# A batched 64x64 matmul: one input loads ahead of the other, two more loads of the other move to ScalarE's queue, ScalarE's order changes, the last tile gets PSUM of its own, and there is one more result buffer

## Chip, cores, metric

One core of a Trainium2 chip. The metric is the device time of one execution in microseconds (us), the median of several. All runs quoted here are fast: none was over 1.5% above the fastest of its kernel. Times in tables of instructions count from the start of the profiled span. The profiled span is shorter than the timed execution by about 2 us. In the lines of the profile DVE is VectorE, ACT is ScalarE, PE is TensorE, POOL is GpSimd and SP is SyncE; the digits in their rows of slices are busy tenths.

## The reference

```python
def setup_inputs():
    return {
        "a": np.random.randn(1024, 64, 64).astype(np.float32),
        "b": np.random.randn(1024, 64, 64).astype(np.float32),
    }

def reference(a, b):
    return np.matmul(a, b).astype(np.float32)
```

There are 1024 products of 64x64 matrices. Inputs are 2 x 16.78 MB, the result 16.78 MB: 50.33 MB over HBM.

## The kernel before

b and the result go in 16 tiles of 64 products (1 MB each), a in 8 tiles of 128 products (2 MB each, read as fp32 and written to SBUF as bf16 by the DMA). I number tiles from 0, so tile 15 is the last of b and of the result, and tile 7 the last of a.

For each tile of the result, VectorE "spreads" the transposed a into a block-diagonal operand, ScalarE casts b to bf16, TensorE multiplies, and the two halves of the result are evacuated (copied to SBUF) from PSUM, where the products are accumulated, the first by ScalarE, the second by VectorE. For each tile of a, VectorE "regroups" it, TensorE transposes it and ScalarE copies the transposes to SBUF. Loads of a and stores of the result are issued by GpSimd and share one DMA queue. Loads of b are issued by SyncE, two of them by ScalarE.

```python
    A_AHEAD = 3; B_AHEAD = 4; N_BD = 2; HOLD = 2
    ...
    o_pool = ctx.enter_context(tc.tile_pool(name="o_pool", bufs=5))
    t_psum = ...(tc.tile_pool(name="t_psum", bufs=4, space=bass.MemoryType.PSUM))
    o_psum = ...(tc.tile_pool(name="o_psum", bufs=2, space=bass.MemoryType.PSUM))
    ...
    def load_a(s):
        a_sb = a_pool.tile([128, 4, 16, 64], bf16, name="a_sb")
        for h in range(4):
            nc.gpsimd.dma_start(out=a_sb[:, h, :, :]..., in_=a_v[s, h])

    def load_b(t):
        b_sb = b_pool.tile([128, 16, 128], fp32, name="b_sb")
        queue = nc.scalar if t in (1, 3) else nc.sync
        queue.dma_start(out=b_sb[:], in_=b_v[t])
    ...
    def multiply(t, between):
        ...
        for half in range(2):
            o_ps = o_psum.tile([128, 4, 2, 2, 64], fp32, name="o_ps")
            for g8 in range(8):
                ...  # 4 matmuls
                if last and g8 % 4 == 3:      # last tile: evacuate quarters
                    gl = g8 // 4 * 2
                    copy = nc.vector.tensor_copy if gl else nc.scalar.copy
                    evacuate(o_ps, 4 * half + gl, gl, 2, copy)
            if not last:
                copy = nc.vector.tensor_copy if half else nc.scalar.copy
                evacuate(o_ps, 4 * half, 0, 4, copy)
            if half == 0:
                between()
        ...  # the tile's store, kept back; the last tile's in quarters

    def advance(t):
        if t + 1 < n_t:
            cast(t + 1)
        if t + B_AHEAD < n_t:
            load_b(t + B_AHEAD)

    with tc.manual_schedule():
        load_a(0)
        for t in range(B_AHEAD):
            load_b(t)
        for bd in bd_tiles:
            nc.vector.memset(bd[:], 0.0)
        ...
        for t in range(n_t):
            s, half = t // 2, t % 2
            if t + 1 < n_t:
                spread(t + 1)
            if half == 0:
                ...  # regroup(s + 2), load_a(s + 4)
            multiply(t, lambda: advance(t))
            ...  # transposes for the next tiles of a
            if t >= HOLD - 1:
                store(t - HOLD + 1)
        ...
```

## Time and profile before

| | before |
|---|---|
| time, median (range) | 139.34 us (139.12 to 139.62) |
| profiled span | 137.7 us |
| VectorE busy | 109.4 us (79%) |
| ScalarE busy | 87.1 us (63%) |
| TensorE matmuls busy | 67.6 us (49%) |
| HBM traffic | 50.33 MB |

Two things are nearly full, and a share of the whole span hides both. First the page's slices: VectorE's and the DMA engines' busy tenths, and what the engines moved in each fortieth of the span.

```profile
DVE  5770034959899999999999999999999999968440
...
DMA  2999999999999999999999999999999999992592
GB/s 61 305 305 308 305 280 260 209 251 273 236 251 298 383 283 267 358 394 356 271 278 387 396 317 268 305 403 390 398 396 400 389 396 389 384 367 106 177 337 100
```

The DMA row is full from the second slice to the 36th (about 124 us), dips, and recovers for the last stores. The GB/s row seems to say that the early slices are slower, but it counts what was written: the loads of a write half of what they read.

The table by stretches of the same kernel (time, then busy us of TensorE, its weight loads, VectorE, ScalarE and GpSimd, granted clock, DMA share, GB/s) puts VectorE beside it:

```profile
60.00:80.00 20.00, 11.87 (x216) 11.02 (x216) 19.35 (x28) 15.31 (x20) 7.13 (x7) 0.82 1.06 345
80.00:100.00 20.00, 13.00 (x218) 12.39 (x216) 19.35 (x27) 15.93 (x21) 4.09 (x3) 0.76 1.05 346
100.00:120.00 20.00, 10.20 (x192) 9.82 (x189) 19.34 (x28) 14.95 (x20) 3.77 (x4) 0.67 1.03 392
120.00:125.00 5.00, 3.62 (x70) 3.51 (x68) 3.86 (x7) 3.46 (x6) 1.09 (x1) 0.50 0.94 357
125.00:130.00 5.00, 2.26 (x40) 2.04 (x38) 3.58 (x7) 2.56 (x7) 1.59 (x2) 0.50 0.25 80
```

VectorE is busy 19.35 of every 20 us, and the DMA engines have no room either, until 125 us. Then the DMA share drops to 0.25.

The start, from the timeline of VectorE (start, duration, instruction, count, idle time before it and what ended it):

```profile
17.17 1.23 DVE L80 COPY a_bf<-a_sb 128x4096 bf16<-128x4096 bf16 x1 [7.76 <-DMA a_sb<-in_a_dram]
...
31.26 1.23 DVE L80 COPY a_bf<-a_sb 128x4096 bf16<-128x4096 bf16 x1 [1.75 <-DMA a_sb<-in_a_dram]
...
35.89 3.09 DVE L102 COPY at_bd<-at_sb 32x1024 f32<-32x1024 f32 x4 [0.59 <-ACT at_sb L92]
```

The first regroup (a's tile 0) is at 17.17 us, the third (a's tile 2) at 31.26 us. From the spread of tile 2 at 35.89 us VectorE runs without a gap for 86.4 us. I call this VectorE's chain.

The end, same view, with GpSimd's issues of stores (POOL):

```profile
119.20 3.10 DVE L102 COPY at_bd<-at_sb 32x1024 f32<-32x1024 f32 x4
...
123.35 0.76 DVE L118 CAST b_bf<-b_sb 128x512 bf16<-128x512 f32 x2 [1.05 <-DMA b_sb<-in_b_dram]
...
124.12 2.79 DVE L146 COPY o_sb<-o_ps 64x512 f32<-64x512 f32 x4
...
127.47 1.59 POOL L135 DMA_DIRECT2D out_dram<-o_sb  x2 [6.38 <-ACT o_sb L146]
...
131.55 1.73 DVE L146 COPY o_sb<-o_ps 64x256 f32<-64x256 f32 x4 [1.74 <-PE o_ps L154]
133.58 0.72 POOL L135 DMA_DIRECT2D out_dram<-o_sb  x1 [2.04 <-DVE o_sb L146]
```

Read it so: the chain's last spread ends at 122.3 us; VectorE waits 1.05 us for b's tile 15; it evacuates its half of tile 14 until 126.9. In the packets, the DMA engines are without load or store from 125.50 to 128.93 us, and the last packet of a store ends at 135.84.

### The profile page before, as it was taken

The page shows a single profiled execution, that of the slowest core. Times are in us where ns is not written, and L with a number is a line of the kernel's source. Part 1 is how long each engine was busy: PE and PEld are TensorE (multiplying, and loading weights), DVE is VectorE, ACT ScalarE, POOL GpSimd, SP SyncE. Part 2 cuts the span into 40 slices and gives each one's busy share as a digit, 9 for nine tenths or more (in the row PEclk, how much of TensorE's full clock was granted, in tenths as well). Part 3 has the DMA queues.
Part 4 walks back from the last instruction along what each step waited for, and adds up shares of the span by engine and source line. Part 5 has one row for each costly group of instructions (what it writes and reads, how often), then busy time and mean ns, then how long its engine had stood idle before and what let it go on. Part 6 is the DMA issues. An engine that isn't in the chain of part 4 may idle for free.

```text
span 137.7 us, 2820 instructions
## 1 busy us (share of the span) xinstructions
PE 67.6 (49%) x1152; PEld 63.9 (46%) x1152; DVE 109.4 (79%) x144; ACT 87.1 (63%) x120; POOL 43.3 (31%) x57
## 2 busy tenths in 40 slices
PE   0000063295857375629563679297229743374510
PEld 0000062295856375619563569296229643373510
DVE  5770034959899999999999999999999999968440
ACT  1030029049899998986799578864996794576400
POOL 6811141743543054205163330213020303210640
PEclk9999999658699959995999555959955995555555
DMA  2999999999999999999999999999999999992592
GB/s 61 305 305 308 305 280 260 209 251 273 236 251 298 383 283 267 358 394 356 271 278 387 396 317 268 305 403 390 398 396 400 389 396 389 384 367 106 177 337 100
DMA packets 17468, 42.12 MB, mean 306 GB/s; under 512 B 1072, under 2 KB 1072, under 8 KB 17456
## 3 DMA queue, kind: packets, MB, share of 16 engines
q0 software_dynamic: 9008, 25.17, 64.4%
q1 hardware_dynamic: 7392, 14.68, 29.8%
q10 hardware_dynamic: 1056, 2.10, 4.1%
q8 instruction: 9, 0.15, 0.4%
q14 instruction: 3, 0.02, 0.0%
HBM read 33.55 MB, written 16.78 MB: 366 GB/s over the span
## 4 chain that ended last, share of the span: by engine, by line
DMA 27%; DVE 20%; SPq 16%; issue 12%; PE 9%; ACT 9%; POOL 3%; POOLq 1%; DVEq 0%; ACTq 0%
SPq L74 16%; DMA b_sb<-in_b_dram 16%; DVE at_bd L102 11%; DMA a_sb<-in_a_dram 10%; DVE o_sb L146 8%; PE at_ps L89 5%; PE o_ps L154 4%; ACT b_bf L113 4%; ACT o_sb L146 3%; ACT at_sb L92 2%; DVE a_bf L80 2%; POOL out_dram L135 2%; POOL a_sb L66 1%; POOLq L241 1%; DVEq L80 0%
## 5 line engine op out<-in xcount | busy, mean ns | idle before, releaser
L154 PE MATMUL o_ps<-b_bf,at_bd 128*128 128x64 bf16 x1024 | 47.0, 217 | 40.4 <-ACT b_bf L113 16.5
L154 PEld LDWEIGHTS <-at_bd 128*128 128x128 bf16 x1024 | 44.9, 114 | 43.8 <-issue 22.5
L102 DVE COPY at_bd<-at_sb 32x1024 f32<-32x1024 f32 x64 | 47.3, 739 | 6.6 <-ACT at_sb L92 4.7
L146 DVE COPY o_sb<-o_ps 64x512 f32<-64x512 f32 (+1 forms) x68 | 44.7, 657 | 4.0 <-PE o_ps L154 1.7
L146 ACT COPY o_sb<-o_ps 64x512 f32<-64x512 f32 (+1 forms) x68 | 37.7, 555 | 14.9 <-PE o_ps L154 11.5
L135 POOL DMA_DIRECT2D out_dram<-o_sb x19 | 20.8, 1096 | 64.9 <-DVE o_sb L146 34.6
L89 PE MATMUL at_ps<-identity,a_bf 128*128 128x128 f32 x128 | 24.1, 353 | 23.4 <-DVE a_bf L80 23.4
L89 PEld LDWEIGHTS at_ps<-identity,a_bf 128*128 128x128 f32 x128 | 20.1, 187 | 23.6 <-issue 23.6
L92 ACT COPY at_sb<-at_ps 128x512 f32<-128x512 f32 x32 | 17.9, 588 | 19.4 <-PE at_ps L89 19.1
L113 ACT CAST b_bf<-b_sb 128x2048 bf16<-128x2048 f32 x15 | 28.5, 1899 | 2.5 <-DMA b_sb<-in_b_dram 2.2
L66 POOL DMA_DIRECT2D a_sb<-in_a_dram x32 | 21.9, 689 | 25.8 <-DMA a_sb<-in_a_dram 22.5
L80 DVE COPY a_bf<-a_sb 128x4096 bf16<-128x4096 bf16 x8 | 9.8, 1227 | 9.7 <-DMA a_sb<-in_a_dram 9.5
L186 DVE MEMSET at_bd<- 128x4096 f32 x2 | 6.9, 3472 | 2.5 <-PEq L230 1.7
L92 ACT ACT_TABLE_LOAD x1 | 1.3, 1283 | 4.8 <-issue 4.8
L74 ACT MOVE_SHAPE b_sb<-in_b_dram x2 | 0.6, 320 | 1.7 <-issue 0.9
L118 DVE CAST b_bf<-b_sb 128x512 bf16<-128x512 f32 x2 | 0.8, 424 | 1.0 <-DMA b_sb<-in_b_dram 1.0
L120 ACT CAST b_bf<-b_sb 128x512 bf16<-128x512 f32 x2 | 1.1, 616 | 0.0
masks.py:199 POOL TENSOR_SCALAR_AFFINE_SELECT identity<-identity 128x128 f32<-128x128 f32 x1 | 0.3, 289 | 0.1
masks.py:197 POOL MEMSET identity<- 128x128 f32 x1 | 0.3, 268 | 0.0
L230 POOL MEMSET const-float32-0.0<- 128x1 f32 x1 | 0.1, 93 | 0.3 <-issue 0.3
L230 POOL MEMSET const-bfloat16-1.0<- 128x1 bf16 x1 | 0.1, 96 | 0.0
L230 POOL MEMSET const-uint8-127<- 128x1 uint8 x1 | 0.1, 96 | 0.0
(1 smaller groups left out, 0.1 us busy)
## 6 DMA issues: line engine op xcount, KB each, us to landing
out_dram<-o_sb POOLq DMA_DIRECT2D x15, 1024.0 KB, 16.9
a_sb<-in_a_dram POOLq DMA_DIRECT2D x32, 256.0 KB, 15.6
out_dram<-o_sb POOLq DMA_DIRECT2D x4, 256.0 KB, 4.8
b_sb<-in_b_dram SPq DMA_DIRECT2D x14, 0.5 KB, 20.2
b_sb<-in_b_dram ACTq DMA_DIRECT2D x2, 0.5 KB, 18.8
```

The costliest lines, as they stand in the source:

```text
L66: nc.gpsimd.dma_start(out=a_sb[:, h, :, :].rearrange("p v k -> p (v k)"), in_=a_v[s, h])
L74: queue.dma_start(out=b_sb[:], in_=b_v[t])
L80: nc.vector.tensor_copy(a_bf[:], a_sb[:].rearrange("p h v k -> p v h k"))
L89: nc.tensor.transpose(at_ps[:, vo, :], a_cols[:, 4 * vo + 2 * j + wl, :], identity[:])
L92: nc.scalar.copy(at_tiles[s][:, j, :, wl, :, :], at_ps[:].rearrange("p vo (g mp) -> p g mp vo", mp=4),)
L102: nc.vector.tensor_copy(bd[rows, :, :, :, h, :].rearrange("p j g wl mo -> p j (g wl) mo"), at_tiles[t // 2][rows, :, half, :, :, :].rearrange(
L113: nc.scalar.copy(b_bf[:], b_sb[:])
L135: nc.gpsimd.dma_start(out=o_v[t, :, lo : lo + n, :], in_=o_sb[:, lo : lo + n].rearrange("p gh j wl n -> p (gh j wl n)"),)
L146: copy(dst, src)
L154: nc.tensor.matmul(o_ps[:, g8 // 2, g8 % 2, j, :], at_bd[:, j, g, :, u], b_bf[:, g, 64 * u : 64 * u + 64], start=(u == 0), stop=(u == 1),)
L186: nc.vector.memset(bd[:], 0.0)
L241: with _tile.TileContext(nc) as tc:
```

## The change

Its intent: let compute start sooner (a's first tile loads alone, and b waits until half of it has landed), feed TensorE sooner (casts ahead of the evacuations on ScalarE), let more loads and stores be in flight (tiles 5 and 7 of b on ScalarE's queue too, six result buffers), and shorten the end (the last tile's quarters in four PSUM banks of their own). One of two memsets goes from VectorE to GpSimd.

```diff
-    o_pool = ctx.enter_context(tc.tile_pool(name="o_pool", bufs=5))
+    o_pool = ctx.enter_context(tc.tile_pool(name="o_pool", bufs=6))
...
-        queue = nc.scalar if t in (1, 3) else nc.sync
-        queue.dma_start(out=b_sb[:], in_=b_v[t])
+        queue = nc.scalar if t in (1, 3, 5, 7) else nc.sync
+        load = queue.dma_start(out=b_sb[:], in_=b_v[t])
+        if t < 2:
+            tc.add_manual_dep(load.ins, first_a[1].ins.name, ...)  # waits for it
...
         for half in range(2):
-            o_ps = o_psum.tile([128, 4, 2, 2, 64], fp32, name="o_ps")
+            if not last:
+                o_ps = o_psum.tile([128, 4, 2, 2, 64], fp32, name="o_ps")
             for g8 in range(8):
+                if last and g8 % 4 == 0:
+                    o_ps = t_psum.tile([128, 2, 2, 2, 64], fp32, name="at_ps")
...
-            if half == 0:
-                between()
...
-        for bd in bd_tiles:
-            nc.vector.memset(bd[:], 0.0)
+        nc.vector.memset(bd_tiles[0][:], 0.0)
...
+        nc.gpsimd.memset(bd_tiles[1][:], 0.0)
...
                 spread(t + 1)
+                cast(t + 1)
+            if t + B_AHEAD < n_t:
+                load_b(t + B_AHEAD)
...
-            multiply(t, lambda: advance(t))
+            multiply(t)
```

More of the change, by code (lines that the diff above doesn't have):

```diff
@@ L60 @@
     a_tiles, b_tiles, abf_tiles, at_tiles, bbf_tiles = {}, {}, {}, {}, {}
-    held = {}
+    held, first_a = {}, []
     def load_a(s):
@@ L65, in load_a @@
         for h in range(4):
-            nc.gpsimd.dma_start(
+            load = nc.gpsimd.dma_start(
                 out=a_sb[:, h, :, :].rearrange("p v k -> p (v k)"), in_=a_v[s, h]
             )
+            if s == 0:
+                first_a.append(load)
         a_tiles[s] = a_sb
@@ L72, in load_b @@
         b_sb = b_pool.tile([128, 16, 128], fp32, name="b_sb")
-        queue = nc.scalar if t in (1, 3) else nc.sync
-        queue.dma_start(out=b_sb[:], in_=b_v[t])
+        queue = nc.scalar if t in (1, 3, 5, 7) else nc.sync
+        load = queue.dma_start(out=b_sb[:], in_=b_v[t])
+        if t < 2:
+            tc.add_manual_dep(
+                load.ins,
+                first_a[1].ins.name,
+                mybir.DependencyInfo(
+                    mybir.DependencyClass.Sync, mybir.DependencyReason.DATA
+                ),
+                reason="first tile of a goes ahead",
+            )
         b_tiles[t] = b_sb
@@ L125, in store, with multiply @@
             piece()
-    def multiply(t, between):
+    def multiply(t):
         at_bd = bd_tiles[t % N_BD][:].rearrange("p j g wl h mo -> p j g (wl h mo)")
@@ L138, in put, with evacuate @@
             )
-        def evacuate(o_ps, gh, gl, n, copy):
+        def evacuate(o_ps, gh, n, copy):
             for par in range(2):
                 for wl in range(2):
-                    src = o_ps[64 * wl : 64 * wl + 64, gl : gl + n, par, :, :]
+                    src = o_ps[64 * wl : 64 * wl + 64, :, par, :, :]
                     dst = o_sb[64 * par : 64 * par + 64, gh : gh + n, :, wl, :]
@@ L148, in multiply @@
         for half in range(2):
-            o_ps = o_psum.tile([128, 4, 2, 2, 64], fp32, name="o_ps")
+            if not last:
+                o_ps = o_psum.tile([128, 4, 2, 2, 64], fp32, name="o_ps")
             for g8 in range(8):
+                if last and g8 % 4 == 0:
+                    o_ps = t_psum.tile([128, 2, 2, 2, 64], fp32, name="at_ps")
                 g = 8 * half + g8
+                gl = (g8 % 4 if last else g8) // 2
                 for j in range(2):
@@ L154, in multiply @@
                         nc.tensor.matmul(
-                            o_ps[:, g8 // 2, g8 % 2, j, :],
+                            o_ps[:, gl, g % 2, j, :],
                             at_bd[:, j, g, :, u],
@@ L161, in multiply @@
                 if last and g8 % 4 == 3:
-                    gl = g8 // 4 * 2
-                    copy = nc.vector.tensor_copy if gl else nc.scalar.copy
-                    evacuate(o_ps, 4 * half + gl, gl, 2, copy)
+                    copy = nc.scalar.copy if g8 == 3 else nc.vector.tensor_copy
+                    evacuate(o_ps, g // 4 * 2, 2, copy)
             if not last:
                 copy = nc.vector.tensor_copy if half else nc.scalar.copy
-                evacuate(o_ps, 4 * half, 0, 4, copy)
-            if half == 0:
-                between()
+                evacuate(o_ps, 4 * half, 4, copy)
         if last:
@@ L173, in multiply @@
             held[t] = [lambda: put(0, 8)]
-    def advance(t):
-        if t + 1 < n_t:
-            cast(t + 1)
-        if t + B_AHEAD < n_t:
-            load_b(t + B_AHEAD)
     with tc.manual_schedule():
```

## The prediction

> **What bounds the kernel now.** Two things run nearly full. (1) DMA: the page's slices show the DMA row at 9 from the second slice to about 123 us. HBM traffic is 33.55 + 16.78 = 50.33 MB. Counting the trace's packets in 4 us windows (a's at the 4 KB that they read), the sum is 392 to 418 GB/s from 5 to 118 us: about 126 us of DMA work, beginning at 2.4 us. (2) VectorE: the table by stretches has it busy 9.7 of every 10 us between 40 and 120 us; per tile 3.09 us of spreads, 2.80 of evacuation, half of a 1.23 us regroup: 6.5 us. PE and ACT have slack. The timeline shows this VectorE chain starting when a's third tile lands (regroup at 31.26 us) and running without a gap to 122.3. Ends: the first tile of a lands at 17.05 us (it shares the engines with b); after 122.3 VectorE loses about 4 us to waits (cast of the last b 1.05, last evacuations 1.17 and 1.74), and the DMA engines idle from 125.5 to 128.9.
>
> **What changes, costed.**
> - Start. a's first packets start at 4.7 us, b's at 2.4. Tile 0 of a alone (2 MB at 400 GB/s) lands near 11 us instead of 17; first transposes 6 us sooner. But about 2.3 us of b traffic (0.7 MB) is given up: about -1.8 us of DMA work. The first three tiles of a and four of b (10.5 MB) land together near 31 us whatever their order, and VectorE's third regroup waits for that: expected at 31.5 to 33 us (31.26 before), so the continuous VectorE chain starts no sooner.
> - One 3.47 us memset leaves VectorE for GpSimd: it lay in waiting time, worth nothing.
> - Casts ahead: PE's waits for the cast (16.5 us in the table of waits) shrink; PE isn't the limit: about 0.
> - Tiles 5 and 7 of b on ACT's queue. The Trainium skill ("DMA: Bandwidth & Descriptors", Queues, rings and completion order) says each DMA engine goes round the queues packet by packet; the trace agrees: per 4 us a moved 0.77 MB against 0.84 for b on two queues, but about 1.02 against 0.55 on one. So b runs ahead by about 8 us: the last b tile lands near 115 us, not 122.9, and the wait for b at the end (2.2 + 1.05 us) goes. Stores lag some 5 us instead; six buffers absorb that.
> - Own PSUM banks: the last tile's matmuls no longer wait (1.6 + 1.6 us) for evacuations; its last evacuation ends near 130.5 instead of 133.3.
>
> **Sum.** VectorE could end 3 us sooner. But stores alone run at only about 330 GB/s (128.9 to 135.8 us), against 397 mixed with loads. With b done at 115, about 6.6 MB of stores remain: 20 us, ending near 135, plus 1.9 us to the end of the span. The DMA tail takes back much of the gain: span about 136 against 137.7, time about 137.6 us (-1.2%).
>
> **Would show it right:** first regroup near 11 us; third still at 31 to 33; last b cast no longer waiting; last tile's matmuls in one unbroken group; DMA idle gap before the last stores shorter than 1.5 us; VectorE still 97% busy from 40 to 120.
>
> **Would make it wrong:** a's third tile landing well before 31 us (more gain, 135); ACT blocked while issuing b loads, or casts blocking evacuations that wait behind them (a loss); a's later tiles lagging so far behind b that regroups wait.
>
> Chances: faster by over 2% 0.25, within 2% 0.70, slower 0.05. Range 135.5 to 139.5 us.

## The result, and the profile after

| | before | after |
|---|---|---|
| time, median (range) | 139.34 us (139.12 to 139.62) | 137.12 us (136.94 to 137.30) |
| ratio, 95% interval | | 0.984 (0.9817 to 0.9863) |
| profiled span | 137.7 us | 134.8 us |
| VectorE busy | 109.4 us | 105.0 us |
| first packet of a / of b | 4.69 / 2.40 us | 2.68 / 11.30 us |
| last packet of a / of b | 90.2 / 122.9 us | 95.3 / 114.6 us |
| end of the store of result tile 5 | 92.8 us | 98.3 us |
| HBM traffic done by 100, 120, 125 us | 38.56, 46.36, 48.18 MB | 38.46, 46.38, 48.18 MB |

A ratio is the mean time of one kernel's fast runs over that of the other's of the same rounds, so it isn't quite the ratio of the medians. The change is 1.6% faster, and the interval lies clear of 1. The time lies in the predicted range, 0.5 us under the predicted 137.6.

The last row is the most telling: for 125 us both kernels move the same bytes in the same time. What the change gained lies behind that.

The slices of the kernel after:

```profile
DVE  5512099069999999997999999997599999999900
...
DMA  2999999999999999999999999999999999998593
GB/s 19 185 204 261 309 305 301 309 308 279 272 294 311 312 394 346 303 275 361 393 360 273 272 381 396 340 267 288 393 394 396 393 399 395 407 406 350 191 320 136
```

The stretches, with the same columns:

```profile
60.00:80.00 20.00, 14.84 (x251) 14.05 (x248) 18.60 (x26) 17.68 (x26) 6.42 (x8) 0.74 1.06 335
80.00:100.00 20.00, 8.77 (x179) 8.17 (x180) 17.18 (x24) 13.39 (x18) 5.33 (x4) 0.86 1.06 346
100.00:120.00 20.00, 13.86 (x240) 12.85 (x239) 19.34 (x27) 15.77 (x24) 5.22 (x4) 0.67 1.03 398
120.00:125.00 5.00, 3.59 (x64) 3.43 (x64) 4.82 (x10) 2.80 (x8) 0.04 (x1) 0.50 0.90 352
125.00:130.00 5.00, 0.00 (x0) 0.00 (x0) 2.83 (x7) 0.13 (x1) 3.69 (x5) 0.50 0.74 242
```

VectorE is no longer full between 60 and 100 us: it now waits, although its chain has the same work. The DMA share between 125 and 130 us is 0.74, not 0.25.

The start of the kernel after, and the wait that came new to VectorE at 95.8 us:

```profile
9.60 1.23 DVE L91 COPY a_bf<-a_sb 128x4096 bf16<-128x4096 bf16 x1 [4.47 <-DMA a_sb<-in_a_dram]
...
28.10 1.23 DVE L91 COPY a_bf<-a_sb 128x4096 bf16<-128x4096 bf16 x1 [4.51 <-DMA a_sb<-in_a_dram]
...
32.17 3.22 DVE L113 COPY at_bd<-at_sb 32x1024 f32<-32x1024 f32 x4
...
95.80 1.23 DVE L91 COPY a_bf<-a_sb 128x4096 bf16<-128x4096 bf16 x1 [2.33 <-DMA a_sb<-in_a_dram]
```

The chain starts 3.7 us sooner (32.17 against 35.89). It gives back 2.33 us waiting for a's tile 7, whose last packet comes 5.1 us later than before.

The end:

```profile
117.71 3.09 DVE L113 COPY at_bd<-at_sb 32x1024 f32<-32x1024 f32 x4
...
120.83 0.77 DVE L129 CAST b_bf<-b_sb 128x512 bf16<-128x512 f32 x2
...
121.63 2.79 DVE L157 COPY o_sb<-o_ps 64x512 f32<-64x512 f32 x4
...
124.45 3.48 DVE L157 COPY o_sb<-at_ps 64x256 f32<-64x256 f32 x8
124.97 3.00 POOL L146 DMA_DIRECT2D out_dram<-o_sb  x4 [5.38 <-issue]
128.23 0.72 POOL L146 DMA_DIRECT2D out_dram<-o_sb  x1 [0.26 <-DVE o_sb L157]
```

There is no wait for b's tile 15 before the cast at 120.83, and the last evacuation ends at 127.93 us instead of 133.28: 5.35 us sooner. But the span ends only 2.9 us sooner. Tile 14's store is issued 2.5 us sooner (124.97 against 127.47): 1.5 us because the chain ends sooner (120.80 against 122.30), 1.05 us because the wait for b's tile 15 is gone. And from there the two kernels take nearly the same time to the end: 9.85 and 10.22 us.

ScalarE's waits of the kernel after (total, times, longest) show what the lagging stores cost it; before, the first of these was 2.3 us:

```profile
ACT o_sb L157 <- DMA out_dram<-o_sb: 5.3, 2, 4.2
```

### The profile page after: what moved, and what is told of

It reads as the page before. It is cut to its first block, busy times and chain, and to the rows that moved or that the text cites. A ratio compares the mean times of both kernels' runs of the same rounds, so it can differ in the third digit from the quotient of the medians.

```text
span 134.8 us, 2815 instructions
## 1 busy us (share of the span) xinstructions
PE 69.3 (51%) x1152; PEld 65.2 (48%) x1152; DVE 105.0 (78%) x143; ACT 84.5 (63%) x122; POOL 46.6 (35%) x58
## 4 chain that ended last, share of the span: by engine, by line
DMA 65%; DVE 18%; issue 9%; POOL 3%; POOLq 1%; DVEq 0%
DMA a_sb<-in_a_dram 48%; DMA out_dram<-o_sb 16%; DVE o_sb L157 10%; DVE at_bd L113 8%; POOL out_dram L146 2%; POOL a_sb L66 1%; POOLq L250 1%; DVE a_bf L91 0%; DVEq L91 0%; POOLq L146 0%; DVEq L113 0%; POOLq L239 0%
## 5 line engine op out<-in xcount | busy, mean ns | idle before, releaser
L169 PEld LDWEIGHTS <-at_bd 128*128 128x128 bf16 x1024 | 45.8, 117 | 41.4 <-DVE o_sb L157 30.7
L169 PE MATMUL o_ps<-b_bf,at_bd 128*128 128x64 bf16 x960 | 44.7, 219 | 36.6 <-DVE o_sb L157 28.7
L113 DVE COPY at_bd<-at_sb 32x1024 f32<-32x1024 f32 x64 | 46.4, 725 | 7.9 <-ACT at_sb L103 5.9
L157 DVE COPY o_sb<-o_ps 64x512 f32<-64x512 f32 x60 | 41.3, 688 | 1.8 <-PE o_ps L169 0.8
L157 ACT COPY o_sb<-o_ps 64x512 f32<-64x512 f32 x60 | 34.8, 580 | 9.5 <-DMA out_dram<-o_sb 5.3
L157 ACT COPY o_sb<-at_ps 64x256 f32<-64x256 f32 x8 | 2.9, 367 | 3.0 <-PE at_ps L169 2.9
L191 DVE MEMSET at_bd<- 128x4096 f32 x1 | 3.5, 3472 | 1.7 <-PEq L239 1.7
L169 PE MATMUL at_ps<-b_bf,at_bd 128*128 128x64 bf16 x64 | 3.6, 241 | 1.2 <-DVE at_bd L113 1.2
L195 POOL MEMSET at_bd<- 128x4096 f32 x1 | 3.5, 3530 | 0.0
L157 DVE COPY o_sb<-at_ps 64x256 f32<-64x256 f32 x8 | 3.4, 421 | 0.1
```

The costliest lines, as they stand in the source:

```text
L113: nc.vector.tensor_copy(bd[rows, :, :, :, h, :].rearrange("p j g wl mo -> p j (g wl) mo"), at_tiles[t // 2][rows, :, half, :, :, :].rearrange(
L157: copy(dst, src)
L169: nc.tensor.matmul(o_ps[:, gl, g % 2, j, :], at_bd[:, j, g, :, u], b_bf[:, g, 64 * u : 64 * u + 64], start=(u == 0), stop=(u == 1),)
L191: nc.vector.memset(bd_tiles[0][:], 0.0)
L195: nc.gpsimd.memset(bd_tiles[1][:], 0.0)
```

## The experiments

Theory A, from the two traces: the DMA engines are full until about 125 us in both kernels. The gain is that tile 14 is evacuated sooner, so that the last two stores (2.1 MB) start sooner; what counts of each part is only what it does to that moment. The rivals: B, the early start is the gain; C, the order of loads is irrelevant; and my prediction's own term, that the last tile's own banks save some 3 us. Each experiment ran 4 to 6 timed times beside the kernel before on the same chip, whose medians were 139.45, 139.40 and 139.42 us in the three groups of four. All results were correct.

This table has what the theory speaks of. "Chain" is the start of the spread of tile 2 and the end of the spread of tile 15 on VectorE. The last column is the span less the time of the store's issue. Profiled columns are of one execution each.

| kernel | time | chain, us | last packet of b | tile 14's store issued | span | to the end |
|---|---|---|---|---|---|---|
| before | 139.34 | 35.89 to 122.30 | 122.91 | 127.47 | 137.69 | 10.2 |
| after | 137.12 | 32.17 to 120.80 | 114.55 | 124.97 | 134.82 | 9.9 |
| after, no wait for b (e1) | 137.10 | 34.90 to 120.95 | 116.23 | 125.12 | 134.97 | 9.9 |
| after, b 5 and 7 on SyncE (e2) | 140.31 | 34.01 to 123.42 | 122.95 | 127.96 | 137.80 | 9.8 |
| after, last tile in o_psum (e3) | 136.98 | 32.17 to 121.24 | 114.38 | 125.39 | 135.29 | 9.9 |
| after, five result buffers (e4) | 140.03 | 33.60 to 124.12 | 114.91 | 128.29 | 138.17 | 9.9 |
| after, casts back (e5) | 136.72 | 32.88 to 120.96 | 115.05 | 125.13 | 134.98 | 9.9 |
| before, with the wait (e6) | 139.75 | 33.85 to 123.48 | 122.80 | 127.63 | 137.59 | 10.0 |
| before, b 5 and 7 and six buffers (e9) | 138.28 | 36.12 to 122.34 | 120.17 | 126.49 | 136.40 | 9.9 |
| before, six buffers (e10) | 139.33 | 36.22 to 122.77 | 122.74 | 127.49 | 137.54 | 10.0 |
| before, b 5 and 7 (e10b) | 139.34 | 36.03 to 123.70 | 119.57 | 127.85 | 137.77 | 9.9 |
| after, tile 14 on ScalarE (e7) | 135.33 | 32.87 to 121.34 | 114.41 | 122.84 | 133.60 | 10.8 |

In the eleven kernels ahead of the last row, the end follows the issue of tile 14's store by 9.8 to 10.2 us, whatever else differs.

### e1: the change without the wait that holds back b

```diff
-        if t < 2:
+        if t < 0:
             tc.add_manual_dep(
```

> The change without the wait that holds back b (all else kept). Theory A (DMA engines full until about 125 us at the same total traffic in both kernels; the gain is only that tile 14 is evacuated 2.5 us sooner, so that the last two stores, 2.1 MB, start sooner): a's first packet goes back from 2.7 to 4.7 us, the first regroup from 9.6 to 17 us, the third from 28.1 to about 31, tile 14's evacuation ends 1 to 3 us later than 124.4, time 0.5 to 2.5 us over the change, but still under the kernel before. Rival B (the early start is the whole gain): time back at 139.3. Rival C (order of loads is irrelevant): time as the change, within 0.4 us.

Measured: 137.10 us (137.04 to 137.33), ratio to before 0.9831 (0.9818 to 0.9844): the time of the change. a's first packet is back at 4.94 us, the first regroup at 17.22, the third at 30.60, as expected. But the chain, which starts 2.7 us later, ends at the same time (120.95), because it has no wait for a's tile 7 on its way. So theory A's number (0.5 to 2.5 us lost) missed and rival B fell. Rival C's number came true here; that the loads' shares do matter, e2 shows. The headline of the change, a's first tile going alone, is worth nothing as the kernel stands: what VectorE gains at the start it gives back waiting later.

### e2: tiles 5 and 7 of b back on SyncE's queue

```diff
-        queue = nc.scalar if t in (1, 3, 5, 7) else nc.sync
+        queue = nc.scalar if t in (1, 3) else nc.sync
```

> The change with tiles 5 and 7 of b back on SyncE's queue. Theory A with b's landing as its lever: b gets a third of the traffic throughout, so the last b tile lands at 123 us or later instead of 114.6, tile 14 and 15 are evacuated as late as before or later, span 137 to 140, time 139 to 142. Rival (VectorE's earlier chain is what counts, b's landing doesn't): time within 0.5 us of the change.

Measured: 140.31 us (139.94 to 140.75), ratio to before 1.0065 (1.0046 to 1.0084): all the gain gone, and slightly slower than before. The last packet of b is at 122.95 us again. With the casts ahead of the evacuations, late b now blocks ScalarE, and what stands behind it in ScalarE's order:

```profile
ACT b_bf L124 <- DMA b_sb<-in_b_dram: 23.5, 9, 5.7
```

and VectorE's spread of tile 14 waits for it too, which the timeline of this run shows:

```profile
114.64 2.83 DVE L113 COPY at_bd<-at_sb 32x1024 f32<-32x1024 f32 x4 [3.42 <-ACT at_sb L103]
```

So two loads on another queue carry 3.2 us. The mechanism is the share of traffic. The Trainium skill ("DMA: Bandwidth & Descriptors", section "Queues, rings and completion order") says that each DMA engine goes round the queues that have work, packet by packet. The trace agrees: with b on two queues, a moved 0.77 MB of reads per 4 us and b 0.84 MB; with b on one, the other queue moved about 1.02 MB and b 0.55 MB. (These figures are from the trace of the kernel before. b's packets are 2 KB; those of a and of the result read or write 4 KB.) A rival would be that SyncE can't issue loads of b any faster. It can: from 117 to 119 us of the kernel before, when few stores were queued, b's one queue moved 293 and then 237 GB/s, against about 138 as its usual share.

### e3: the last tile back in the PSUM buffers of the others

```diff
-            if not last:
-                o_ps = o_psum.tile(...)
+            o_ps = o_psum.tile(...)
...
-                if last and g8 % 4 == 0:
-                    o_ps = t_psum.tile([128, 2, 2, 2, 64], fp32, name="at_ps")
```

> The change with the last tile back in the two buffers of the other tiles. Theory A: its second half waits for VectorE's evacuation of tile 14 (ends 124.4 us), its last evacuation ends at about 128.2 instead of 127.9; time as the change within 0.5 us, because the DMA tail sets the end. Rival (my prediction's term: own banks save some 3 us at the end): time 2 to 3 us over the change.

Measured: 136.98 us (136.85 to 137.07), ratio 0.9819 (0.9806 to 0.9831). The last evacuation ends at 130.37 us, 2.4 us later than in the change (I expected 0.3 us), and the time doesn't move. The DMA engines have two stores to write by then, and reach the last quarter no sooner. The own banks do shorten the compute at the end, and are worth nothing in this kernel.

### e4: five result buffers

```diff
-    o_pool = ...(tc.tile_pool(name="o_pool", bufs=6))
+    o_pool = ...(tc.tile_pool(name="o_pool", bufs=5))
```

> The change with five result buffers. As stores lag now (tile 5's store done at 98.3 us, 92.8 before), ScalarE's evacuations wait for stores from tile 6 on, longest about 9 us at tile 10, and VectorE's chain is pushed back. Theory A: tile 14's evacuation ends 2 to 6 us later, time 139 to 142. Rival (traffic is the limit, so a lagging chain is caught up while stores drain): time within 0.7 us of the change.

Measured: 140.03 us (140.01 to 140.41), ratio 1.0043 (1.003 to 1.0057). Both engines now wait for stores to free a buffer; VectorE never did in the change:

```profile
ACT o_sb L157 <- DMA out_dram<-o_sb: 12.6, 3, 5.6
...
DVE o_sb L157 <- DMA out_dram<-o_sb: 3.5, 2, 2.2
```

The chain ends 3.3 us later, tile 14's store is issued 3.3 us later, the time is 2.9 us longer. As expected, though the longest wait was 5.6 us, not 9.

### e5: casts and loads of b back behind the first half's evacuation

```diff
...                                   # in multiply, and a new advance(t): as in the kernel before
+            if half == 0:
+                between()
...
                 spread(t + 1)
-                cast(t + 1)
-            if t + B_AHEAD < n_t:
-                load_b(t + B_AHEAD)
...
-            multiply(t)
+            multiply(t, lambda: advance(t))
```

> The change with cast and load of b back behind the evacuation of a tile's first half. ScalarE has slack, so by theory A time as the change within 0.5 us. Rival (the early casts feed the matmuls and so carry the gain): 1 us or more over the change.

Measured: 136.72 us (135.93 to 137.21), ratio 0.98 (0.9773 to 0.9827). This interval overlaps that of the change (0.9817 to 0.9863): no difference shown. As in e1 the chain ends at the same 121 us.

### e6: the kernel before with only the wait

```diff
...                                   # first_a is filled in load_a, as in the change
-        queue.dma_start(out=b_sb[:], in_=b_v[t])
+        load = queue.dma_start(out=b_sb[:], in_=b_v[t])
+        if t < 2:
+            tc.add_manual_dep(load.ins, first_a[1].ins.name, ...)
```

> The kernel before with only the wait that lets the first tile of a go ahead. By theory A a's tiles land sooner (third regroup at 29 to 30 us instead of 31.3), but b starts 8.5 us later on one and a half queues, so that its last tiles land no sooner than 122.9 us and hold the end: time 139.4 to 140.6. Rival (the start is the gain): 137.1 to 138.3.

Measured: 139.75 us (139.62 to 140.31), ratio 1.0032 (1.0015 to 1.005), as expected: the third regroup comes at 29.79 us, the last of b at 122.80. Rival B falls a second time.

### e9, e10, e10b: two one-line edits in the kernel before, together and each alone

```diff
-    o_pool = ...(tc.tile_pool(name="o_pool", bufs=5))      # e9, e10
+    o_pool = ...(tc.tile_pool(name="o_pool", bufs=6))
-        queue = nc.scalar if t in (1, 3) else nc.sync       # e9, e10b
+        queue = nc.scalar if t in (1, 3, 5, 7) else nc.sync
```

> The kernel before with only two edits: tiles 5 and 7 of b on ScalarE's queue, and six result buffers. Theory A': these two parts are the whole gain (b's last tile lands at about 115 us, the end is the issue of tile 14's store + 9.9 us); time within 0.6 us of the change (137.1), last b tile at 112 to 117 us, tile 14's store issued at 124.5 to 125.5. Rival (they need the other parts): 138.3 or more.

> The kernel before with six result buffers and nothing else. Before, the only wait for a result buffer is 2.3 us of ScalarE that VectorE doesn't feel: time as before within 0.5 us (138.9 to 139.9). Rival (buffers are the gain by themselves): 138.3 or less.

> The kernel before with tiles 5 and 7 of b on ScalarE's queue and nothing else. b runs ahead and stores lag, with only five result buffers: last b tile near 120 us as with the two edits, but ScalarE and VectorE wait for stores; time 139.0 to 141. Rival (b's queue is the gain by itself): 138.3 or less, as with both edits.

Measured: together (e9) 138.28 us (138.00 to 138.34), ratio 0.9914 (0.9893 to 0.9935); six buffers alone 139.33 us, ratio 0.9994 (0.9979 to 1.0009); the queue alone 139.34 us, ratio 1.0004 (0.9987 to 1.0021). Each alone is nothing, as expected; the two together are half of the gain. Why: with the queue alone, b's last packet comes at 119.57 us, but ScalarE waits 5.8 us for result buffers, and the chain ends at 123.70. With the buffer alone, b still lands at 122.74 us.

My expectation for e9, the whole gain, fell (b's last packet came at 120.17 us, not by 117; tile 14's store was issued at 126.49, not by 125.5). What is missing shows at the start: in e9, as before, VectorE's spread of tile 2 waits for ScalarE, where a cast and an evacuation stand ahead of it. The first such lines of the two timelines, e9 and then e1:

```profile
36.12 3.10 DVE L102 COPY at_bd<-at_sb 32x1024 f32<-32x1024 f32 x4 [1.05 <-ACT at_sb L92]
```

```profile
34.90 3.17 DVE L113 COPY at_bd<-at_sb 32x1024 f32<-32x1024 f32 x4 [0.26 <-ACT at_sb L103]
```

From there e9's chain takes 86.2 us and that of e1 86.1 us. e1 has the early casts and no wait for b; e5 has the wait and no early casts; both reach the full gain. So either of the two brings the chain's start to 34.9 us or sooner, and a start still sooner brings nothing. That these two parts do it is the simplest reading of e1, e5 and e9; it wasn't isolated further. The memset was never taken back alone, but the traces speak against it: in e9 and in e1 VectorE waits for a's tile 0 after its memsets, and regroups it at 17.2 us. And ScalarE's timelines show the step: in e9 it idles 1.12 us, evacuates at 30.70 us and casts at 33.09; in e1 it casts first, at 29.62.

### e7: tile 14 evacuated by ScalarE alone

```diff
-                copy = nc.vector.tensor_copy if half else nc.scalar.copy
+                copy = nc.vector.tensor_copy if half and t < n_t - 2 else nc.scalar.copy
```

> The change with all of tile 14's evacuation on ScalarE, which sits idle from 119.2 to 121.9 us. Theory A says that the end follows the issue of tile 14's store by 9.9 us as long as the DMA engines have run dry by then: the store's issue moves from 125.0 to about 122.7, VectorE's last evacuation from 127.9 to about 126.3, and the gap in DMA traffic at 125 us closes; span 132.5 to 133.3, time 134.8 to 135.6. Rival (the end is set by the whole traffic, not by this issue): under 0.5 us of gain.

Measured: 135.33 us (135.25 to 135.70), ratio to before 0.9711 (0.9687 to 0.9735), in the expected range (the span, 133.60 us, is just over the expected 132.5 to 133.3): 1.8 us faster than the change, by medians of different groups. Tile 14's store moves to where theory A put it:

```profile
120.20 2.36 ACT L157 COPY o_sb<-o_ps 64x512 f32<-64x512 f32 x4 [0.47 <-PE o_ps L169]
...
122.84 0.89 POOL L146 DMA_DIRECT2D out_dram<-o_sb  x1 [2.72 <-ACT o_sb L157]
```

In 1 us steps from 124 us, the packets of the change moved 221, 37, 143 and 348 GB/s; in e7 311, 356, 336 and 344. The hole is closed. The end comes 10.8 us after the issue here, not 9.9, since the engines still had older stores to write. VectorE's last evacuation ends sooner too (126.81 us, 127.93 in the change), but e3 shows that this end isn't what counts.

### e8: e7, with tile 14's store split, and the last tile's stores on SyncE's queue

```diff
...                                   # and e7's edit
+            queue = nc.sync if last else nc.gpsimd
-            nc.gpsimd.dma_start(
+            queue.dma_start(
...
         if last:
             held[t] = [lambda q=q: put(2 * q, 2) for q in range(4)]
+        elif t == n_t - 2:
+            held[t] = [lambda: put(0, 4), lambda: put(4, 4)]
```

> As the run before it, and tile 14 is stored in two halves and the last tile's four quarters go out on SyncE's queue beside GpSimd's. The first half of tile 14 is ready at 119.2 us. If one queue with few stores holds the tail to 320 GB/s, two queues lift it: 0.3 to 1.2 us faster than the run with ScalarE alone, time 133.8 to 135.2. If the tail's rate is the same on two queues: no gain over that run.

Measured: 135.29 us (135.20 to 135.62), ratio 0.9701 (0.9679 to 0.9724): no gain over e7 (135.33). On SyncE's queue the stores went out in packets of 1 KB, and their four issues took 4.78 us.

### e11: e7, with an edit meant to lighten VectorE from tile 9 on, which did nothing

```diff
...                                   # and e7's edit
-                    copy(dst, src)
+                    if copy is nc.vector.tensor_copy and n == 4 and t >= 9 and par + wl == 2:
+                        nc.scalar.copy(dst, src)
+                    else:
+                        copy(dst, src)
```

> As the run with tile 14 on ScalarE, and from tile 9 on ScalarE takes one more of the eight evacuation copies of a tile, so VectorE's chain is lighter by 0.69 us in each of tiles 9 to 13, 3.4 us in all. If that chain sets when the last two stores begin and traffic isn't yet the limit, the store of tile 14 is issued 1.5 to 3.4 us sooner and the time falls by 0.5 to 1.2 us, to 134.1 to 134.8; the DMA tail then stays near 400 GB/s. Rival (traffic or ScalarE is the limit by now): within 0.4 us of that run or slower.

Measured: 135.25 us (135.12 to 135.58), ratio 0.9705 (0.9689 to 0.9722). But the edit never took effect: the trace has VectorE still doing four copies per tile, because the Python test compares a bound method by identity, which is never true. So this is a second run of e7, which it repeats within 0.1 us, and says nothing of a lighter VectorE. Whether that would still help is open.

## Why the prediction was right or wrong

**What bounds the kernel: right.** The DMA engines and VectorE are both full until 120 to 125 us; the traffic done by 125 us is the same 48.18 MB in both kernels.

**"About 2.3 us of b traffic (0.7 MB) is given up": wrong.** I took a's first packet at 4.7 us as fixed. It is at 2.68 us when b isn't loading (2.67 to 2.71 in every kernel with the wait), and at 4.69 to 5.24 when b is (before, e1, e9, e10, e10b). The DMA engines started 0.3 us later than before, not 2.3.

**"Land together near 31 us whatever their order", third regroup at 31.5 to 33 us: wrong in the step.** It came at 28.10 us: a had the engines alone until b's first packet at 11.30 us, so three tiles of a were done at 27.2 us and four of b at 32.8. (The first regroup, predicted near 11 us, came at 9.60.) What I concluded from it, that the early start is worth little, e1 shows to hold, for another reason: the 2.7 us by which the chain starts sooner than in e1 are lost again before 121 us, above all to the wait for a's tile 7.

**Memset worth nothing:** not tested alone, but the traces bear it out: e6 keeps both memsets on VectorE beside the wait, and its first regroup still waits 0.66 us for a's tile 0. **Casts ahead about 0:** right inside the change (e5); in the kernel before with the two edits, either they or the wait for b make some 1.2 us (e1, e5 and e9).

**b's queue: right.** Last packet of b predicted near 115 us, measured 114.55; stores predicted to lag 5 us, measured 5.6 (tile 5). VectorE's wait for b at the end went; ScalarE still waits 1.9 us for b's tile 15, at 115.2 us, where VectorE doesn't feel it. This step, with the sixth buffer, is the core of the gain (e2, e4). "Six buffers absorb that" was right for VectorE; ScalarE's waits for a buffer still rose from 2.3 to 5.3 us. I didn't predict that five buffers would lose all of it.

**Own banks: they shorten the compute, and the time doesn't need it.** I had the last evacuation at 130.5 us; it was at 127.93, because the chain was sooner. e3 takes the banks away: the last evacuation moves by 2.4 us and the time not at all.

**"The DMA tail takes back much of the gain": right, and the sizes were off.** Of 5.35 us sooner at the last evacuation, 2.9 us reached the span. But "stores alone run at only about 330 GB/s" was wrong for most of that stretch: from 117 to 123 us, with stores queued up, they ran at 403 GB/s, and only the last 4 us at 324. (Nor did the trace before show just 330: over the whole of 128.9 to 135.8 us it gives about 303, with the gaps between the last stores in it.) So the 6.2 MB left at b's last packet (predicted 6.6) ended at 133.0 us, not 135. Against that, the engines didn't stay full: they ran short around 125 us while tile 14's store wasn't issued yet (I expected a gap under 1.5 us; adding up what the 1 us steps from 124 to 127 lack of 400 GB/s gives 2.0 us). And I expected VectorE 97% busy from 40 to 120 us; it was 94%, and 86% between 80 and 100. These errors partly cancel, so the time came out closer than its terms. That is luck: with the fast stretch, the gap and the slow end, 6.16 MB took 18.5 us, which is 334 GB/s, the assumed rate for another reason. And two of the three things that the prediction said would make it wrong did happen: a's third tile landed well before 31 us, and a later tile of a lagged until a regroup waited for it (2.33 us). They nearly cancelled.

What stays open: why the stores slow down for the last 2 MB (e8's second queue brought no gain), and whether VectorE's chain or the traffic limits e7. On the first the trace after shows this much: from 117 to 123 us a 4 KB packet of a store took 165 ns (median), from 129 us on 192 ns, with all 16 engines at work in both. On the second: from 5 to 131.7 us e7's packets have no gap of over 0.2 us.

## What to carry to other kernels

With the DMA engines full, making the first load arrive sooner only moved a wait here (e1, e6); look also at the moment when the last large store can be issued, and move work so that it comes sooner (e7: one line, 1.8 us). The number of queues that a stream used set its share of the full DMA engines here, and the stream that got more made another lag: give the lagging one the buffers in the same edit, since here each of the two edits alone was worth nothing and together they were half of the gain.

## What the Trainium skill lacked or had wrong

- "DMA: Bandwidth & Descriptors", section "Issuing engines are not separate DMA queues", says that issuing from several engines "will only save the time on the sequencer it takes to initiate the DMA". Here two of 16 loads on another engine's queue moved b's last packet from 122.95 to 114.55 us and the time by 3.2 us (e2). The total rate stayed near 400 GB/s; what moved is b's share of it. The page's own section on arbitration implies it, but draws no such conclusion.
- The same page, "Queues, rings and completion order", says that the turns are by packet, and not that packet size then sets the shares: with b on one queue, b's 2 KB packets got 0.55 MB where the other queue's 4 KB packets got about 1.02 MB.
- The same page, "Specifications", gives a first byte latency of about 1 us for GpSimd's DMAs. From the issue at 1.28 us to a's first packet it was 1.4 us alone and 3.4 us where loads of b had been issued 0.5 us ahead (before); b's first packet came 4.3 us after its issue when it followed a (7.04 to 11.30), and 1.6 us after it when it was first. No page gives a first byte time for a stream that starts behind another.
- The same page, "Specifications", gives an HBM limit of about 358 GB/s for a core, half of a stack's 716. Reads and writes together ran at 385 to 418 GB/s here, with the other cores unused by this program, so the row alone misleads for a core by itself. Further down the page itself keeps that figure for both cores of a pair at work.
- No page has what the last stores did here: 403 GB/s from 117 to 123 us, 324 GB/s in the last 4 us. That few were left can't be the whole reason: e7's ran at 336 to 344 GB/s from 126 to 129 us with several queued.
